# Ten quartered groups and four whole feature tiles in each feed-forward input product, instead of nine and eight

## The chip, the cores and the metric

The kernel runs on one core of one Trainium2 chip. The metric is the device time of one execution in microseconds. The engines are named as in the profile: PE (TensorE, matrix multiplication; PEld is its weight load), DVE (VectorE), ACT (ScalarE), POOL (GpSimd) and SP (SyncE, which here only issues DMAs). L604 means line 604 of the kernel before the change.

## The reference

Two layers work on 512 tokens of 1,024 features. Each has two feed-forward blocks (FFN) around a mixer, and a gated embedding at its end:

```python
def swiglu_ffn(x, w_in, w_out):
    g, u = jnp.split(x @ w_in, 2, axis=-1)
    return (jax.nn.silu(g) * u) @ w_out
...
    for i in range(DEPTH):
        h = h + 0.5 * swiglu_ffn(rms_norm(h, ffn1_norm[i]), ffn1_w_in[i], ffn1_w_out[i])
        ...
        h = h + jnp.concatenate([y_ssd, y_mla.astype(y_ssd.dtype)], axis=-1) @ w_out_mix[i]
        h = h + 0.5 * swiglu_ffn(rms_norm(h, ffn2_norm[i]), ffn2_w_in[i], ffn2_w_out[i])
        gate = jax.nn.sigmoid(rms_norm(h, ple_norm[i]) @ w_ple_gate[i])
        h = h + gate * (p[i] @ w_ple_proj[i])
    return rms_norm(h, final_norm)
```

`w_in` is 1,024 x 5,632: 2,816 columns for g and 2,816 for u. `w_out` is 2,816 x 1,024. All is float32. The change touches the input product `x @ w_in` of the four FFNs alone.

## The kernel before

**Layout.** Activations lie transposed: features on the 128 partitions, the 512 tokens along the free dimension. The 1,024 features of h are eight row tiles; g and u have 22 feature tiles of 128 columns each.

**Three matmuls for one.** Every operand is split into a high and a low half (float32r), and a product is three matmuls: high by high, high by low, low by high. A weight tile is split by one cast on ACT (L306) and one subtraction on DVE (L307), activations in `halves` by L443 and L444. Weights are loaded by SP into six raw buffers (L289); three pairs of buffers take the split ones. `weights` hands out the next unit and calls the splits of the two units after it.

**Whole tiles.** `whole(x, f)` multiplies one feature tile of g or u in the plain way: eight row tiles, three matmuls each of 512 columns (L430 to L432), 24 matmuls into one bank.

**Groups by quarters.** Four feature tiles at a time can be made with seven products instead of eight (Winograd's form of Strassen's scheme): the weight columns, the rows and the tokens are each cut in two. `product(bank, n, p, first)` is one of the seven, p from 1 to 7: four row tiles, two feature tiles and three matmuls of 256 columns (L604 to L606), 24 in all. Products 1, 2 and 4 take the normalised input itself. Products 5, 3, 6 and 7 take sums of its quarters, which `norm.sums(j)` makes for row tiles 2j and 2j + 1 (L560 to L566 on DVE, with two scaled copies on ACT, L551, and the halves of four results). On the weights' side, product 5 takes product 1's raw weights plus another quarter (an addition on DVE, L318); product 6 takes product 5's raw weights plus product 3's (L318 again); product 4 takes product 6's, and product 7 product 3's, with a further quarter added while it is loaded (an accumulating DMA on POOL's queue, L323). So the weights of 5, 6, 4 and 7 depend on earlier ones in the same buffer. Product 3 accumulates into product 5's bank, product 6 into product 1's, and 7 and 4 into the bank after 6. Results are combined on DVE (L633), with copies on ACT (L628), and `finish` multiplies by the norm's factor and applies SiLU (g, L620 and L621), or multiplies with the finished g (u, L624).

**Order of an FFN's input product.** Four whole tiles of g; the norm's statistics (L502, from the sum of squares that L490 and L491 make), their spread over the partitions (L526, L528) and the first results' evacuation (L671, L675) lie between, and one `sums(j)` after each whole tile. Then nine groups: u 0 to 3, then g and u in turn for tiles 4 to 7 and so on up to 16 to 19. `ORDER` gives the order of the products in a group; products 7 and 4 are put off into the next group. At the end, around the last group's products 7 and 4, g 20, g 21, u 20 and u 21 go whole. Each finished pair of hidden tiles is split into halves (`split_pair`) as early as buffers allow (`presplit`), the last by `split_last`. The output product follows: eight tiles, each in three pieces of 8, 8 and 6 hidden tiles (L769, L776, L778).

**What sets the order on the engines.** The calls in the code do not fix it alone: the framework that builds the program (`schedule_with_timeline_sim=True`, L1583) puts each engine's instructions in order by its own estimate of when they are ready, earlier calls first among the ready. On the chip each engine then works in that order.

## Time and profile before

| what | us |
|---|---|
| median of three runs | 2308.51 |
| lowest and highest | 2308.25 and 2312.47 |
| the profiled execution | 2306.83 |
| its span, first to last instruction | 2305.1 |

| engine | busy us | share of the span |
|---|---|---|
| PE | 2278.3 | 99% |
| DVE | 1563.9 | 68% |
| ACT | 1094.2 | 47% |
| POOL | 212.9 | 9% |

A row of a timeline has the start in us, the time taken, the engine, the line, the operation, what it writes and reads by the names in the code with its shape, and how many of the same kind follow one another; behind it in brackets stands the idle time of the engine before it and what ended that. A row of the waits has who waited for whom, the total in us, how often, and the longest. A row of the windows has a stretch, its length, each engine's busy time in it with its instructions, PE's granted clock, and what the DMA engines did. In the costliest groups: count, busy us, mean ns of one, then the idle time before them and its cause.

### The profile page before, as it was taken

What the parts mean: (1) busy time and instruction counts of PE and PEld (TensorE: products, weight loads), DVE (VectorE), ACT (ScalarE), POOL (GpSimd) and SP (SyncE); (2) the same over time, 40 slices, a digit from 0 to 9 for tenths busy, and PEclk for the clock granted to TensorE, in tenths of its full rate; (3) what the DMA queues carried; (4) which work ended last, traced back from release to release, by engine and by line L of the source; (5) the groups of instructions that cost most, each with busy time, mean ns of one, the idle gap of its engine ahead of it and who ended that gap; (6) DMA issues with size and microseconds to landing.
All of it is one profiled execution on the core that took longest, in us unless ns stands there. A gap on an engine that the chain in (4) does not pass through costs nothing.

```text
span 2305.1 us, 34208 instructions
## 1 busy us (share of the span) xinstructions
PE 2278.3 (99%) x13542; PEld 2010.8 (87%) x13542; DVE 1563.9 (68%) x2456; ACT 1094.2 (47%) x1780; POOL 212.9 (9%) x208
## 2 busy tenths in 40 slices
PE   8999999999999999999999999999999999999998
PEld 7999888888888899988899998888788889998887
DVE  7878445688676877733777773476876778776345
ACT  7456324455454645522554552254544555454224
POOL 1110001132000111000011100012310001110000
PEclk9999999999999999999999999999999999999999
DMA  6666334311222566623356652332112126664232
GB/s 173 160 155 154 89 98 114 87 43 51 62 66 74 135 156 159 151 76 89 105 130 157 161 140 84 104 106 78 35 45 83 59 78 156 162 159 119 87 87 74
DMA packets 360428, 247.89 MB, mean 108 GB/s; under 512 B 20590, under 2 KB 354636, under 8 KB 360268
## 3 DMA queue, kind: packets, MB, share of 16 engines
q1 hardware_dynamic: 322252, 207.96, 30.4%
q0 software_dynamic: 38016, 37.75, 10.8%
q8 instruction: 106, 1.74, 0.3%
q14 instruction: 54, 0.44, 0.1%
HBM read 243.58 MB, written 2.10 MB: 107 GB/s over the span
## 4 chain that ended last, share of the span: by engine, by line
PE 70%; issue 23%; DVE 3%; DMA 1%; ACT 1%; SPq 1%; POOL 1%; POOLq 0%; DVEq 0%; ACTq 0%
PE b L432 15%; PE b L430 15%; PE b L431 14%; PE b L606 5%; PE b L604 5%; PE b L605 5%; PE b L439 1%; PE b L438 1%; PE b L440 1%; DMA raw<-in_ffn_w_in_dram 1%; PE b L1126 1%; DVE lo L307 1%; PE b L1291 1%; PE b L1110 0%; PE b L502 0%
## 5 line engine op out<-in xcount | busy, mean ns | idle before, releaser
L306 ACT CAST hi<-raw 128x1024 fp32r<-128x1024 f32 (+3 forms) x536 | 524.2, 979 | 838.7 <-PE b L431 411.3
L307 DVE TENSOR_TENSOR lo<-raw,hi 128x1024 fp32r<-128x1024 f32 (+3 forms) x536 | 613.6, 1145 | 405.6 <-ACT hi L306 403.9
L430 PE MATMUL b<-s,hi 128*128 128x512 f32 (+1 forms) x1754 | 692.4, 397 | 6.0 <-ACT hi L306 5.9
L432 PE MATMUL b<-s,lo 128*128 128x512 f32 (+1 forms) x1754 | 684.5, 391 | 3.9 <-DVE lo L307 3.9
L431 PE MATMUL b<-s,hi 128*128 128x512 f32 (+1 forms) x1754 | 683.1, 390 | 0.0
L604 PE MATMUL b<-s,hi 128*128 128x256 f32 x2016 | 569.8, 283 | 1.6 <-ACT hi L306 1.6
L605 PE MATMUL b<-s,hi 128*128 128x256 f32 x2016 | 569.7, 283 | 0.0
L606 PE MATMUL b<-s,lo 128*128 128x256 f32 x2016 | 565.2, 284 | 0.0
L430 PEld LDWEIGHTS b<-s,hi 128*128 128x128 f32 x1754 | 329.8, 188 | 75.0 <-ACT hi L306 8.9
L432 PEld LDWEIGHTS b<-s,lo 128*128 128x128 f32 x1754 | 329.2, 188 | 74.7 <-DVE lo L307 6.6
L604 PEld LDWEIGHTS b<-s,hi 128*128 128x128 f32 x2016 | 387.3, 192 | 3.4 <-ACT hi L306 2.9
L431 PEld LDWEIGHTS b<-s,hi 128*128 128x128 f32 x1754 | 329.7, 188 | 67.6 <-issue 2.9
L605 PEld LDWEIGHTS b<-s,hi 128*128 128x128 f32 x2016 | 387.3, 192 | 0.3
L606 PEld LDWEIGHTS b<-s,lo 128*128 128x128 f32 x2016 | 384.5, 192 | 0.2
L323 POOL DMA_DIRECT2D raw<-in_ffn_w_in_dram x72 | 92.7, 1287 | 586.2 <-DVE lo L307 567.7
L516 POOL TENSOR_TENSOR nr<-nv,half 128x4 f32<-128x4 f32 (+1 forms) x14 | 18.3, 1304 | 1041.0 <-DVE nv L508 921.7
L443 ACT CAST s<-b 128x128 fp32r<-128x128 f32 (+2 forms) x196 | 66.9, 361 | 99.8 <-DVE s L444 33.8
L443 ACT CAST s<-s 128x256 fp32r<-128x256 f32 (+1 forms) x248 | 94.5, 423 | 32.4 <-DVE s L624 15.8
L444 DVE TENSOR_TENSOR s<-s,s 128x256 fp32r<-128x256 f32 (+1 forms) x248 | 99.7, 447 | 4.5 <-ACT s L443 4.0
L444 DVE TENSOR_TENSOR s<-b,s 128x128 fp32r<-128x128 f32 (+2 forms) x196 | 75.3, 402 | 32.2 <-ACT s L443 30.9
L318 DVE TENSOR_TENSOR raw<-raw,raw 128x1024 f32<-128x1024 f32 x72 | 88.1, 1224 | 1.8
L438 PE MATMUL b<-hi,s 128*128 128x512 f32 (+1 forms) x208 | 78.1, 375 | 0.0
(245 smaller groups left out, 2248.0 us busy)
## 6 DMA issues: line engine op xcount, KB each, us to landing
raw<-in_ffn_w_in_dram SPq DMA_DIRECT2D x176, 512.0 KB
raw<-in_ffn_w_in_dram POOLq DMA_DIRECT2D x72, 512.0 KB, 5.9
raw<-in_ffn_w_out_dram SPq DMA_DIRECT2D x64, 512.0 KB
raw<-in_w_in_mix_dram SPq DMA_DIRECT2D x50, 512.0 KB
raw<-in_w_out_mix_dram SPq DMA_DIRECT2D x32, 512.0 KB
raw<-in_ffn_w_out_dram SPq DMA_DIRECT2D x32, 384.0 KB
raw<-in_w_ple_gate_dram SPq DMA_DIRECT2D x16, 512.0 KB
raw<-in_w_q_b_dram SPq DMA_DIRECT2D x16, 192.0 KB
```

Of the source, the lines that this page charges most:

```text
L306: A.copy(hi[:, :n], x[:, :n])
L307: V.tensor_tensor(lo[:, :n], x[:, :n], hi[:, :n].bitcast(F32), op=ALU.subtract)
L323: lambda dst, src: G.dma_start(out=dst, in_=src, accum_op=ALU.add))
L430: mm(b, lhsT=hi[:, kk, cs], rhs=xh, start=st, stop=False)
L431: mm(b, lhsT=hi[:, kk, cs], rhs=xl, start=False, stop=False)
L432: mm(b, lhsT=lo[:, kk, cs], rhs=xh, start=False, stop=en)
L438: mm(b, lhsT=xh[:, cs], rhs=hi[:, kk], start=first, stop=False)
L443: A.copy(hi, src)
L444: V.tensor_tensor(lo, src, hi.bitcast(F32), op=ALU.subtract)
L604: mm(o, lhsT=hi[:, k, cs], rhs=xh, start=first and f == k == 0, stop=False, **more)
L605: mm(o, lhsT=hi[:, k, cs], rhs=xl, start=False, stop=False, **more)
L606: mm(o, lhsT=lo[:, k, cs], rhs=xh, start=False, stop=f == 1 and k == 3, **more)
```

## The change

The groups become ten: g 2 to 5, u 0 to 3, g 6 to 9, u 4 to 7, and so on to g 18 to 21 and u 16 to 19. Only g 0 and g 1 go whole at the beginning, and u 20 and u 21 at the end, around the last group's products 7 and 4. The sums for row tiles 4 to 7 are called after the second whole tile, behind the spread and the evacuation. In the first group product 2 comes before product 5 instead of after it. The g of the last pair of tiles is now made in a group, so u 20 and u 21 are multiplied into it as they come (`last_evac`), and the last pair is split like the others; `presplit` is called seven times around the end instead of ten, and counts with all 22 tiles.

```diff
-GROUPS = [("u", 0)] + [(x, q) for q in range(1, KF // 4) for x in "gu"]
+GROUPS = [(x, f + 2 * (x == "g")) for f in range(0, KF - 2, 4) for x in "gu"]
...
-FIRST_ORDER = ((1, 0), (5, 0), (2, 0), (3, 0), (6, 0))
+FIRST_ORDER = ((1, 0), (2, 0), (5, 0), (3, 0), (6, 0))
...
-        for f in range(4):
+        for f in range(2):
             whole("g", f)
         for n in range(NG):
             for p, back in ORDER if n else FIRST_ORDER:
                 quarter_unit(n - back, p)
         quarter_unit(NG - 1, 7)
-        whole("g", LAST)
+        whole("u", KF - 2)
         quarter_unit(NG - 1, 4)
-        whole("g", LAST + 1)
-        whole("u", LAST)
-        whole("u", LAST + 1)
+        whole("u", KF - 1)
...
-                if q < done[0] and len(slots.free) - 4 - (LAST - len(hid[0]) * 2) >= KEEP:
+                if q < done[0] and len(slots.free) - 4 - (KF - len(hid[0]) * 2) >= KEEP:
...
-        for f in range(4):
+        def last_evac(f, b):
+            for a in range(2):
+                x = hid[a][-1][:, f * HT:(f + 1) * HT]
+                V.tensor_tensor(x, b[:, a * HT:(a + 1) * HT], x, op=ALU.mult)
+            banks.put(b)
+
+        for f in range(2):
             held.append((f, whole("g", f)))
             if f == 0:
                 start()
                 norm.stats()
-            if f == 2:
-                norm.spread()
-            if f >= 2:
-                while held:
-                    evac(*held.pop(0))
             norm.sums(f)
+        norm.spread()
+        while held:
+            evac(*held.pop(0))
+        norm.sums(2)
+        norm.sums(3)
...
-                    done[0] = (n + 1) // 2 * 2
+                    done[0] = n // 2 * 2
...
-        g = [whole("g", LAST)]
+        b = whole("u", KF - 2)
+        last_evac(0, b)
         presplit(2)
         product(ba, NG - 1, 4, False)
         finish(NG - 1, 1, 0, ba.ap)
         banks.put(ba)
-        done[0] = LAST // 2
-        presplit(1)
-        g.append(whole("g", LAST + 1))
+        done[0] = KF // 2 - 1
         presplit(2)
-        for f in range(2):
-            t = S()
-            V.tensor_tensor(t.ap, g[f].ap, norm.rb.ap, op=ALU.mult)
-            banks.put(g[f])
-            A.activation(t.ap, t.ap, AF.Silu)
-            b = whole("u", LAST + f)
-            if f:
-                norm.drop(rb=False)
-            V.tensor_tensor(t.ap, b.ap, t.ap, op=ALU.mult)
-            banks.put(b)
-            hid[f].append(t)
-            presplit(2)
...
+        b = whole("u", KF - 1)
+        norm.drop(rb=False)
+        last_evac(1, b)
+        done[0] = KF // 2
+        presplit(2)
```

## The prediction, on record before the changed kernel was timed

> **What bounds the kernel now.** I read the page first (busy shares, granted clock, chain), then PE's waits, then the timelines of PE and DVE at the four places where an FFN (a feed-forward block) begins, and at one where its input product ends.

> ```profile
> PE 2278.3 (99%) x13542; PEld 2010.8 (87%) x13542; DVE 1563.9 (68%) x2456; ACT 1094.2 (47%) x1780; POOL 212.9 (9%) x208
> PEclk9999999999999999999999999999999999999999
> PE 70%; issue 23%; DVE 3%; DMA 1%; ACT 1%; SPq 1%; POOL 1%; POOLq 0%; DVEq 0%; ACTq 0%
> PE b L430 <- ACT hi L306: 5.9, 6, 1.4
> PE b L432 <- DVE lo L307: 3.9, 7, 1.3
> PE b L1526 <- DMA s<-in_x_dram: 3.6, 3, 1.6
> ```

> PE is busy for 99% of the span at an undiminished clock and makes up most of the chain; its longest wait is 1.6 us, its waits for weight splits (ACT's high half, DVE's low half) 10 us in all. So it is PE's work that counts, unless another engine falls behind it somewhere. What PE takes is read from rhythms, since its matmuls overlap and their mean times do not add:

> ```profile
> 825.26 1.23 DVE L318 TENSOR_TENSOR raw<-raw,raw 128x1024 f32<-128x1024 f32 x1
> ...
> 845.42 1.23 DVE L318 TENSOR_TENSOR raw<-raw,raw 128x1024 f32<-128x1024 f32 x1
> ...
> 1009.01 0.69 DVE L776 SCALAR_TENSOR_TENSOR raw<-b,s 128x512 f32<-128x512 f32 x1 [1.96 <-PE b L432]
> ...
> 1023.97 0.69 DVE L776 SCALAR_TENSOR_TENSOR raw<-b,s 128x512 f32<-128x512 f32 x1 [1.96 <-PE b L432]
> ```

> The first two rows are the same step of two neighbouring groups: a group of seven products, 7 x 24 = 168 matmuls of 256 columns, takes 20.16 us, 120.0 ns a matmul, 2.88 us a product. The other two are output tiles of 22 x 3 = 66 matmuls of 512 columns: 14.96 us, 226.7 ns a matmul, so a whole feature tile (24) takes 5.44 us.

> **The change on PE.** Each of four FFNs loses four whole tiles (21.76 us) and gains a group (20.16 us): 1.60 us less, 6.4 us in all. That is what seven products for eight leave once the narrow matmul pays its extra: two of 256 columns take 240.0 ns against 226.7 for one of 512.

> [...]

> **What rides along.**

> ```profile
> L307 DVE TENSOR_TENSOR lo<-raw,hi 128x1024 fp32r<-128x1024 f32 (+3 forms) x536 | 613.6, 1145 | 405.6 <-ACT hi L306 403.9
> L323 POOL DMA_DIRECT2D raw<-in_ffn_w_in_dram x72 | 92.7, 1287 | 586.2 <-DVE lo L307 567.7
> raw<-in_ffn_w_in_dram POOLq DMA_DIRECT2D x72, 512.0 KB, 5.9
> core 0: us, PE busy (x) PEld busy (x) DVE busy (x) ACT busy (x) POOL busy (x), PEclk, DMA share, GB/s
> 739.00:772.00 33.00, 30.80 (x133) 24.36 (x132) 33.00 (x62) 25.25 (x46) 0.00 (x0) 1.00 0.30 93
> 28.60:41.70 13.10, 11.24 (x57) 8.95 (x56) 13.10 (x30) 8.14 (x17) 0.00 (x0) 1.00 0.38 121
> 1155.00:1182.00 27.00, 27.00 (x141) 23.02 (x140) 19.79 (x34) 14.42 (x23) 1.92 (x1) 1.00 0.32 101
> 949.40:985.40 36.00, 34.75 (x176) 29.29 (x175) 23.39 (x40) 17.61 (x32) 0.00 (x0) 1.00 0.43 125
> ```

> A group brings seven weight splits for the four of the whole tiles, two additions of weights (L318), four loads on SP for four that go, and two accumulating loads on POOL's queue (72 become 80; 1.3 us to issue, 5.9 to land). In a steady group all of this is hidden: the 20.16 us is exactly the matmuls' time, and the added group is one more such. Its cover is the product of the neighbour group that runs meanwhile; it is missing at the end of the last group, as before. I cost it at nothing; uncovered, a landing would cost up to its 5.9 us once per FFN.

> At the end two whole tiles instead of four lie around the last two products, and only eight of eleven pairs of hidden tiles are split into halves in call order before the output product starts. The first matmul that needs the other three comes two whole tiles, two products and two output pieces (each 5.44 us) after the last group, 27.5 us, plus the wait that stands there now:

> ```profile
> PE b L430 <- ACT hi L306: 0.7, 1, 0.7
> PE b L432 <- DVE lo L307: 0.5, 1, 0.5
> ...
> 963.25 1.77 DVE L444 TENSOR_TENSOR s<-s,s 128x256 fp32r<-128x256 f32 x5
> ```

> DVE was busy 23.39 of the 36.00 us that follow the last group now, and loses two weight splits (2 x 1.145). It fits with 6 us to spare, so I cost this end at nothing. If the order defeats that, three pairs, 12 subtractions of 0.35 us (five take 1.77), cost up to 4 us per FFN. A gain is bounded by the 1.2 us of those two waits.

> **Where it can lose: the beginning.** Product 5 needs sums of the normalised input from all eight row tiles, each a chain of DVE and ACT steps, and its own weights, made by an addition (L318), a cast and a subtraction. Today PE has four whole tiles and product 1 to do meanwhile; after the change two whole tiles and products 1 and 2. Nothing can overtake product 5 on PE: product 3 accumulates into its bank, product 6 takes its raw weights, the next group follows. After product 5 begins, the changed kernel has 144 narrow matmuls more and 48 wide ones less to run, 17.28 - 10.88 = 6.4 us. So product 5 must begin 6.4 us earlier than now to break even, and 8.0 us earlier for the full 1.60 us.

> ```profile
> 768.41 1.23 DVE L307 TENSOR_TENSOR lo<-raw,hi 128x1024 fp32r<-128x1024 f32 x1
> 769.54 0.77 DVE L444 TENSOR_TENSOR s<-s,s 128x256 fp32r<-128x256 f32 x2
> 770.21 0.70 DVE L491 TENSOR_TENSOR s<-s,raw 128x512 f32<-128x512 f32 x1
> 770.81 1.23 DVE L318 TENSOR_TENSOR raw<-raw,raw 128x1024 f32<-128x1024 f32 x1
> ...
> 774.07 1.00 PE L502 MATMUL b<-ones,s 128*128 128x64 f32 x8
> 774.89 0.37 PE L605 MATMUL b<-s,hi 128*128 128x256 f32 x1
> 775.09 0.28 PE L606 MATMUL b<-s,lo 128*128 128x256 f32 x1
> ```

> This is the second FFN of layer 0. The row at 775.09 is the 15th of product 1's 24 matmuls, so product 5 begins 10 x 0.12 later, at 776.3, and must begin by 769.9. But DVE has no idle moment from 739 to 772 (33.00 of 33.00 above). When it is done, at 772.04, it has made all sums, the weights up to product 1's (768.41) and product 5's addition. The changed order gives it one subtraction less up to there (g0, g1, products 1 and 2 for g0 to g3 and product 1; 1.13 us from row to row), to 770.9, and then product 5's own 1.13, since its split is called after the last sums: 772.0. (Product 2, now ahead of product 5, leaves its result to an addition on DVE that is called after that split and stands behind it.) The low half is needed for the third matmul only: 771.8, 1.9 us late. That is the upper bound. The lower is no wait, -1.6. I take the upper bound less what product 1's subtraction overtook in these rows, two steps of the sums and one of the squares (769.54 to 770.81, 1.27 us): +0.6. The same FFN of layer 1 has the same order: +1.2 together.

> ```profile
> 23.23 0.69 DVE L491 TENSOR_TENSOR s<-s,raw 128x512 f32<-128x512 f32 x1
> 28.56 0.22 DVE L789 CAST pf<-pos_i 4x128 f32<-4x128 int32 x1 [4.63 <-DMA pos_i<-in_positions_dram]
> ...
> 41.30 0.40 DVE L444 TENSOR_TENSOR s<-s,s 128x256 fp32r<-128x256 f32 x1
> ...
> 42.09 1.00 PE L502 MATMUL b<-ones,s 128*128 128x64 f32 x8
> 42.90 0.37 PE L604 MATMUL b<-s,hi 128*128 128x256 f32 x1
> ```

> In the first FFN product 5 begins at 42.90; break-even is 36.5. DVE stands 4.63 us for a small load, then works without a gap (13.10 of 13.10) until the last sum at 41.70. By the same steps product 5 would start at 41.5, 5.0 us late. If moved weight work fills the 4.63 us, 0.4 late; a wholly free start is -1.6. Between 0.4 and 5.0 no row is nearer; I take the middle, 2.7.

> ```profile
> 1163.93 0.99 DVE L444 TENSOR_TENSOR s<-s,s 128x256 fp32r<-128x256 f32 x2
> 1167.91 1.23 DVE L307 TENSOR_TENSOR lo<-raw,hi 128x1024 fp32r<-128x1024 f32 x1 [2.99 <-ACT hi L306]
> ```

> At the first FFN of layer 1 the sums end by 1164.9, DVE idles 2.99 us, and PE is busy 27.00 of 27.00 us: no backlog, so the full -1.6 (at worst 0).

> **The sum.** -1.6 + 1.2 + 2.7 = +2.3 us. The profiled execution took 2306.83 (span 2305.1 and 1.7 around it), which gives 2309.1; the median of the runs is 2308.51, 1.68 higher, and so 2310.8. A measurement tells a change from none beyond about 0.2%, 4.6 us: I forecast no difference, 2304 to 2313 for this case.

> **Rivals.**
> (1) The starts do not lose: ACT and DVE slip product 5's split in among the sums (for it: they overtake already at 768.41; against: DVE has no gap there). Then 4 x -1.6 = -6.4: 2302.1.
> (2) Slower: DVE, which works through its queue in order, does all sums before product 5's subtraction. Both bounds hold: -1.6 + 2 x 1.9 + 5.0 = +7.2: 2315.7. It decides once that subtraction ends over 1 us past 771 in the second FFN, or at 40 or later in the first. For it speaks the call order; against it only the row at 768.41.
> (3) The clock falls. In the forecast's first FFN PE is through with what precedes product 5 at 34.9 (1.6 ahead of break-even) and waits until 39.2: 4.3 us, longer than any wait now (1.6), and no row shows what that does to the clock. [...]

> **Chances.** Forecast 0.43; (1) 0.27, because the margin between it and the forecast is in the order of a queue that I cannot see; (2) 0.25; (3) 0.05. So faster 0.27, same 0.43, slower 0.30. The range goes from just below (1) to just above (2): 2301.5 to 2317. It leaves out a late end of the input product and a start better than free.

> **What would show it.** 2016 matmuls of L604 become 2240 with the group's rhythm still 20.16 us. At the second FFN's start product 5 should begin near 770.5 with a wait of PE for a split just before; in the first FFN near 39.2 after some 4 us of idle PE; none at layer 1's first FFN. If PE waits there for nothing, (1) is right; if product 5 starts after 771.8 or 41.5, or the output product waits for hidden tiles, I am wrong on the other side.

## The result, and the profile after

The changed kernel took 2323.11 us, median of four runs (2321.68 to 2326.61), beside 2310.06 for the kernel before in the same comparison (2308.25 to 2312.47): ratio 1.0060, 95% interval 1.0048 to 1.0071. It is slower by 0.6%, about 13 us. The forecast was no difference, 2310.8, with a range up to 2317. The profiled executions have spans of 2305.1 and 2321.5 us: 16.4 apart, more than the medians, since that of the kernel before (2306.83) is the shortest of 26 (median 2310.45), and the longer ones have a lower mean granted clock (0.996 to 0.998 from 2310.44 us on). Lines of the changed kernel are three lower around the splits (L303 the cast, L304 the subtraction, L315 the addition of weights) and the products (L601 to L603); the whole tiles are L427 to L429, `sums` L557 to L563, the halves L440 and L441, the squares L488, the statistics L499.

From the page of after, the engines and PE's granted clock:

```profile
PE 2280.3 (98%) x13830; PEld 2025.6 (87%) x13830; DVE 1594.9 (69%) x2496; ACT 1112.8 (48%) x1812; POOL 223.2 (10%) x216
PEclk9999999999999999999999999999999999999999
```

PE is still busy for 98%, and in tenths of full speed the clock looks untouched. Neither row tells anything: the loss lies in a few spots of some microseconds. PE's waits in after (total, times, longest) show it first:

```profile
PE b L601 <- ACT hi L303: 10.1, 9, 2.3
PE b L603 <- DVE lo L304: 7.2, 5, 2.5
PE b L427 <- ACT hi L303: 3.9, 4, 1.7
PE b L429 <- DVE lo L304: 2.1, 4, 0.5
```

The products now wait 17.3 us for their splits, up to 2.5 us at a time. Before, they waited 1.6 us in all:

```profile
PE b L604 <- ACT hi L306: 1.6, 3, 0.5
```

To place the loss I took, for every matmul of a product or a whole tile, the time from its start to the next start beyond 0.1200 or 0.2267 us: gaps over 0.25 us are waits, smaller ones are slow matmuls. Each FFN is counted from 20, 740, 1140 or 1880 us, so with the end of the mixer in front of it. The end of an FFN is its last output tile on DVE (L776, after: L760). First and last start of that line, before and after:

```profile
L776 DVE SCALAR_TENSOR_TENSOR raw<-b,s x32: 691/692/693, 261.5 to 2236.2; 128x512 f32<-128x512 f32 x32
```

```profile
L760 DVE SCALAR_TENSOR_TENSOR raw<-b,s x32: 691/692/692, 269.6 to 2252.6; 128x512 f32<-128x512 f32 x32
```

| FFN | waits, us | slow matmuls, us | fewer matmul us | sum | its end moved by |
|---|---|---|---|---|---|
| first, layer 0 | 3.74 to 11.39 | 1.23 to 3.65 | -1.60 | +8.5 | +8.1 |
| second, layer 0 | 4.26 to 7.48 | 1.11 to 2.88 | -1.60 | +3.4 | +3.3 |
| first, layer 1 | 1.69 to 2.85 | 0.54 to 0.52 | -1.60 | -0.5 | -0.5 |
| second, layer 1 | 4.30 to 8.77 | 1.11 to 3.80 | -1.60 | +5.6 | +5.4 |

The sums explain the whole 16.4 us within 0.6: 16.5 us more of waits, 6.9 us of matmuls at a slower rhythm, 6.4 us saved. In the two second FFNs 3.1 to 3.2 us of the added waits and 1.7 to 1.8 of the slowness lie at the beginning; in layer 1 another 1.28 and 0.95 lie at the end of the input product.

The second FFN of layer 0 in after, PE's timeline (start, time taken; in brackets the idle time and what ended it):

```profile
771.57 0.39 PE L601 MATMUL b<-s,hi 128*128 128x256 f32 x1
771.79 0.28 PE L602 MATMUL b<-s,hi 128*128 128x256 f32 x1
773.00 0.39 PE L601 MATMUL b<-s,hi 128*128 128x256 f32 x1 [0.93 <-ACT hi L303]
773.22 0.28 PE L602 MATMUL b<-s,hi 128*128 128x256 f32 x1
775.96 0.39 PE L603 MATMUL b<-s,lo 128*128 128x256 f32 x1 [2.46 <-DVE lo L304]
...
776.84 0.41 PE L602 MATMUL b<-s,hi 128*128 128x256 f32 x1
777.05 0.41 PE L603 MATMUL b<-s,lo 128*128 128x256 f32 x1
...
782.84 1.00 PE L499 MATMUL b<-ones,s 128*128 128x64 f32 x8
783.65 0.37 PE L601 MATMUL b<-s,hi 128*128 128x256 f32 x1
```

The first pair of rows is product 2, the second product 5; both run out of operands after two matmuls, and PE stands until product 2's low half is there at 775.9. Behind the wait the matmuls come every 0.21 us instead of every 0.12. DVE at that place:

```profile
769.25 1.23 DVE L315 TENSOR_TENSOR raw<-raw,raw 128x1024 f32<-128x1024 f32 x1
770.39 0.77 DVE L441 TENSOR_TENSOR s<-s,s 128x256 fp32r<-128x256 f32 x2
771.06 0.69 DVE L488 TENSOR_TENSOR s<-s,raw 128x512 f32<-128x512 f32 x1
771.66 1.43 DVE L441 TENSOR_TENSOR s<-s,s 128x256 fp32r<-128x256 f32 x4
...
774.67 1.23 DVE L304 TENSOR_TENSOR lo<-raw,hi 128x1024 fp32r<-128x1024 f32 x1
775.81 0.70 DVE L488 TENSOR_TENSOR s<-s,raw 128x512 f32<-128x512 f32 x1
776.41 2.37 DVE L304 TENSOR_TENSOR lo<-raw,hi 128x1024 fp32r<-128x1024 f32 x2
...
782.96 1.24 DVE L304 TENSOR_TENSOR lo<-raw,hi 128x1024 fp32r<-128x1024 f32 x1
```

DVE has no idle moment from 747.1 to 784.2. The addition of weights that the prediction feared (L315) is early; product 2's subtraction (774.67) is late, behind twelve steps of sums and squares, and those of products 5 and 3 follow at 776.41. Product 6's, at 782.96, is late as well: PE works on product 6 ahead of product 3 (which needs product 5's bank, copied at 784.97 by ACT), and product 6's first matmul with a low half starts at 784.25, 0.05 us after that subtraction ends. The granted clock in after, by windows (length, busy times with instructions, clock, DMA share, GB/s), and the same time in before:

```profile
32.30:39.20 6.90, 5.95 (x29) 5.81 (x28) 6.90 (x13) 5.13 (x12) 0.00 (x0) 0.51 0.24 78
776.40:779.90 3.50, 3.50 (x19) 3.50 (x18) 3.50 (x7) 1.04 (x2) 0.00 (x0) 0.51 0.49 150
1916.50:1919.90 3.40, 3.40 (x19) 3.40 (x18) 3.40 (x7) 0.88 (x2) 0.00 (x0) 0.50 0.53 159
2114.50:2117.90 3.40, 2.88 (x7) 2.31 (x8) 3.40 (x8) 2.78 (x7) 0.00 (x0) 0.50 0.65 190
```

```profile
776.40:779.90 3.50, 3.50 (x32) 3.50 (x31) 1.98 (x3) 2.14 (x3) 1.89 (x2) 1.00 0.50 159
```

The clock halves at four of the places with new waits (0.50 and 0.51 in these windows), for 3.4 us or twice that; in 3.5 us PE starts 19 matmuls instead of 32 there. Not every new wait has this behind it: the one of 1.20 us in the first FFN of layer 1, at 1189.0, has none (1.00 from 1185 to 1200).

### The profile page after: what moved, and what is told of

It reads as the page before. It is cut to its first block, busy times and chain, and to the rows that moved or that the text cites. A ratio compares the mean times of both kernels' runs of the same rounds, so it can differ in the third digit from the quotient of the medians.

```text
span 2321.5 us, 34922 instructions
## 1 busy us (share of the span) xinstructions
PE 2280.3 (98%) x13830; PEld 2025.6 (87%) x13830; DVE 1594.9 (69%) x2496; ACT 1112.8 (48%) x1812; POOL 223.2 (10%) x216
## 3 DMA queue, kind: packets, MB, share of 16 engines
q8 instruction: 108, 1.77, 0.3%
## 4 chain that ended last, share of the span: by engine, by line
PE 58%; issue 33%; DVE 3%; DMA 2%; POOL 1%; ACT 1%; SPq 1%; POOLq 0%; ACTq 0%
PE b L429 15%; PE b L427 15%; PE b L428 15%; DMA raw<-in_ffn_w_in_dram 2%; PE b L435 2%; PE b L436 2%; PE b L437 2%; POOL raw L320 1%; PE b L1110 1%; DVE lo L304 1%; PE b L1275 1%; ACT hi L303 0%; PE b L1301 0%; PE b L1251 0%; PE b L1248 0%
## 5 line engine op out<-in xcount | busy, mean ns | idle before, releaser
L303 ACT CAST hi<-raw 128x1024 fp32r<-128x1024 f32 (+3 forms) x548 | 536.9, 981 | 842.6 <-PE b L428 390.8
L304 DVE TENSOR_TENSOR lo<-raw,hi 128x1024 fp32r<-128x1024 f32 (+3 forms) x548 | 628.1, 1147 | 416.0 <-ACT hi L303 411.9
L601 PE MATMUL b<-s,hi 128*128 128x256 f32 x2240 | 636.2, 285 | 11.7 <-ACT hi L303 10.1
L427 PE MATMUL b<-s,hi 128*128 128x512 f32 (+2 forms) x1626 | 641.9, 397 | 3.9 <-ACT hi L303 3.9
L603 PE MATMUL b<-s,lo 128*128 128x256 f32 x2240 | 630.1, 285 | 7.4 <-DVE lo L304 7.2
L429 PE MATMUL b<-s,lo 128*128 128x512 f32 (+2 forms) x1626 | 635.0, 391 | 2.1 <-DVE lo L304 2.1
L602 PE MATMUL b<-s,hi 128*128 128x256 f32 x2240 | 634.4, 284 | 0.0
L428 PE MATMUL b<-s,hi 128*128 128x512 f32 (+2 forms) x1626 | 633.4, 390 | 0.0
L601 PEld LDWEIGHTS b<-s,hi 128*128 128x128 f32 x2240 | 432.5, 193 | 15.7 <-ACT hi L303 13.3
L603 PEld LDWEIGHTS b<-s,lo 128*128 128x128 f32 x2240 | 429.4, 193 | 9.1 <-DVE lo L304 8.9
L602 PEld LDWEIGHTS b<-s,hi 128*128 128x128 f32 x2240 | 432.3, 193 | 0.6
L429 PEld LDWEIGHTS b<-s,lo 128*128 128x128 f32 (+1 forms) x1626 | 305.5, 188 | 67.3 <-DVE lo L304 4.2
L427 PEld LDWEIGHTS b<-s,hi 128*128 128x128 f32 (+1 forms) x1626 | 305.7, 188 | 66.8 <-ACT hi L303 4.7
L428 PEld LDWEIGHTS b<-s,hi 128*128 128x128 f32 (+1 forms) x1626 | 305.6, 188 | 62.6 <-issue 2.9
L440 ACT CAST s<-b 128x128 fp32r<-128x128 f32 (+2 forms) x196 | 67.1, 362 | 99.7 <-DVE s L441 33.8
L440 ACT CAST s<-s 128x256 fp32r<-128x256 f32 (+1 forms) x256 | 94.1, 416 | 27.2 <-DVE s L620 10.6
L315 DVE TENSOR_TENSOR raw<-raw,raw 128x1024 f32<-128x1024 f32 x80 | 98.0, 1225 | 6.4 <-DMA raw<-in_ffn_w_in_dram 4.2
L441 DVE TENSOR_TENSOR s<-s,s 128x256 fp32r<-128x256 f32 (+1 forms) x256 | 100.6, 438 | 1.4 <-ACT s L440 0.7
L441 DVE TENSOR_TENSOR s<-b,s 128x128 fp32r<-128x128 f32 (+2 forms) x196 | 75.3, 402 | 32.2 <-ACT s L440 30.9
L513 POOL TENSOR_TENSOR nr<-nv,half 128x4 f32<-128x4 f32 (+1 forms) x14 | 19.2, 1373 | 722.8 <-DVE nv L505 722.1
## 6 DMA issues: line engine op xcount, KB each, us to landing
raw<-in_ffn_w_in_dram SPq DMA_DIRECT2D x176, 512.0 KB
raw<-in_ffn_w_in_dram POOLq DMA_DIRECT2D x80, 512.0 KB, 5.9
raw<-in_ffn_w_out_dram SPq DMA_DIRECT2D x64, 512.0 KB
raw<-in_w_in_mix_dram SPq DMA_DIRECT2D x50, 512.0 KB
raw<-in_w_out_mix_dram SPq DMA_DIRECT2D x32, 512.0 KB
raw<-in_w_ple_gate_dram SPq DMA_DIRECT2D x16, 512.0 KB
```

Source lines behind the costliest of these rows:

```text
L303: A.copy(hi[:, :n], x[:, :n])
L304: V.tensor_tensor(lo[:, :n], x[:, :n], hi[:, :n].bitcast(F32), op=ALU.subtract)
L427: mm(b, lhsT=hi[:, kk, cs], rhs=xh, start=st, stop=False)
L428: mm(b, lhsT=hi[:, kk, cs], rhs=xl, start=False, stop=False)
L429: mm(b, lhsT=lo[:, kk, cs], rhs=xh, start=False, stop=en)
L440: A.copy(hi, src)
```

## The experiments

The theory after the result, called B: at the beginning of an FFN DVE's queue is the bound, and the change takes away 10.88 us of whole-tile work per FFN that ran while DVE caught up. Rivals: the split buffers (product 2 must wait until g 0 has left one of three pairs), the order of products or of sums, the half clock, and in the first FFN DVE's stop for a small load. Letters of theories belong to the expectation that they stand in. Ratios are to the kernel before on the same chip, in brackets their 95% intervals.

**Order of the first products.**

```diff
-FIRST_ORDER = ((1, 0), (2, 0), (5, 0), (3, 0), (6, 0))
+FIRST_ORDER = ((1, 0), (5, 0), (2, 0), (3, 0), (6, 0))
```

> The changed kernel with the first group's old order, product 5 ahead of product 2. If product 5's sums are what is late (as the prediction had it), PE waits longer, 2 to 3 us more at each of three FFNs: 2328 to 2332. If product 2's and 5's weight splits are late together (A, C), the order of the two makes no difference: within 3 us of 2323.

2323.26 us, 1.0054 (1.0039 to 1.0070). The swap of products 2 and 5 makes no difference that can be measured, for either sign.

**Sums for row tiles 4 to 7 called between products 2 and 5.**

```diff
-        norm.sums(2)
-        norm.sums(3)
...
+                    if n == 0:
+                        norm.sums(2)
+                        norm.sums(3)
                     bb = B()
                     product(bb, n, 5, True)
```

> The changed kernel, with the sums for row tiles 4 to 7 called between products 2 and 5 of the first group, so that the weight splits of products 2, 5 and 3 stand ahead of those sums in call order. Theory A (the splits of products 2 and 5 stand behind the sums in DVE's order, and that order makes PE wait): at both second FFNs the 5.5 us that PE waits in products 2 and 5 falls under 3 us, the clock stays whole there, and the time falls by 4 to 8 us against the changed kernel, to 2315 to 2319. Rival B (DVE has too much to do in total, the order only moves the wait): the wait turns up at product 5, 3 or 6 and the time stays within 3 us of 2323. Rival C (the cast of product 2's weights waits for a buffer that product 1 releases): the cast stays where it is, and only DVE's 3 us behind it go.

2322.00 us, 1.0052 (1.0034 to 1.0071). In the second FFNs the trace has the same steps on DVE in the same order, so this try did not move what it was to move, presumably because the framework puts ready steps first wherever they are called. It decides nothing.

**Useless work for PE.** 24 discarded wide matmuls per FFN (all but layer 1's first), and then 12 (with `norm.ops[4:]`):

```diff
+        if (i, nm) != (1, "f1"):
+            b = B()
+            for k, (xh, xl) in enumerate(norm.ops[:8]):
+                for x in (xh, xl, xh):
+                    mm(b.ap, lhsT=ident_r, rhs=x, start=True, stop=True)
+            banks.put(b)
         cur = {}
```

> The changed kernel with 24 matmuls of 512 columns more (5.44 us of PE), called behind the second whole tile in three of the four FFNs (not in the first FFN of layer 1); their result is thrown away. If the loss at the beginning is PE standing idle (all theories of the start), they lie in the wait: at the two second FFNs the time stays within 1 us or falls by up to 1.7 us each, because the clock need not drop; in all 2318 to 2325. If PE's own work sets the time there, 3 x 5.44 us come on top: 2339.

2322.34 us, 1.0052 (1.0036 to 1.0068): 3 x 5.44 = 16.3 us of added matmuls cost nothing. At the second FFNs' beginnings waits and slow matmuls fall from 8.4 us to 2.4 and 2.8 (same count as above), by about as much as the added work, and the clock stays whole there (1.00 from 745 to 801 in layer 0).

> The changed kernel with 12 discarded wide matmuls (2.7 us of useless PE work, half of those tried before) between g 1 and product 1 in all FFNs but the first of layer 1. Theory K (the half clock costs time of its own): the waits for product 2's split shrink from 3.7 to about 1 us, the clock does not fall there, and the 1.7 us that the half clock took come back in each second FFN, more useless work making the kernel faster: 2317 to 2320. Rival: the half clock falls into time that PE would have waited anyway, and DVE sets the pace until product 6: 2322 to 2324.

2323.78 us, 1.0057 (1.0044 to 1.0069). The waits shrink by 2.4 us (5.8 to 3.4 in each second FFN), but the clock still falls to 0.50, from 777.2 and from 1917.3. So the expected gain did not come, and the half clock could not be taken away by itself: the 24 matmuls that kept it up took as long as wait and half clock together. What it costs alone stays open.

**Three whole tiles at the beginning.** u 20 goes whole after g 1 and is kept in a slot; u 21 stays at the end:

```diff
+        b = whole("u", KF - 2)
+        first = S()
+        A.copy(first.ap, b.ap)
+        banks.put(b)
         norm.spread()
...
-        b = whole("u", KF - 2)
-        last_evac(0, b)
+        last_evac(0, first)
+        slots.put(first)
```

> The changed kernel with tile 20 of u whole at the beginning instead of at the end (its result kept in a buffer), so three whole tiles at the beginning and one at the end. If cover at the beginning is what is missing, the waits of 5.5 us at the second FFNs and the clock's drops there go, the first FFN loses 3 to 5 us less, and the time is 2304 to 2311, under or at the kernel before. Rival: the end lacks the cover instead, products 7 and 4 wait for their accumulating loads (up to 5.9 us per FFN), and the time is 2315 or more.

2311.55 us, 1.0001 (0.9992 to 1.0011): one whole tile moved to the beginning takes the loss back in the sum, though not the saving. The ends of the FFNs stand +3.7, +3.2, -1.0 and -0.9 us against before, each by itself. So the second FFN of layer 0 gets nothing back: PE's 3.7 us of waits at products 2 and 5 become 1.3 us there, at products 1 and 2, but it then waits 0.8 us for product 6's cast (781.49) and 1.65 us for POOL's step of the norm (L513, at 783.64), and the clock is at 0.50 from 783.6 to 787.0.

**Four at the beginning**, none at the end (u 21 moved likewise):

```diff
+        firsts = []
+        for f in range(2):
+            b = whole("u", KF - 2 + f)
+            t = S()
+            A.copy(t.ap, b.ap)
+            banks.put(b)
+            firsts.append(t)
...
```

> Ten groups as in the changed kernel, but g 0, g 1, u 20 and u 21 all go whole at the beginning, u 20 and u 21 kept in two slots until the last g is there; none goes whole at the end. Theory: the loss is the missing cover at the beginning, and four whole tiles give all of it back, so that the 1.6 us that each FFN's matmuls save come through, less one wait at an end that now has only products 7 and 4: 2305 to 2308, faster than before. Rival: the saving does not exist on the chip (the group's narrow matmuls cost it elsewhere, or the uncovered end takes over 2 us in each FFN): 2311 or more.

2327.92 us, 1.0077 (1.0063 to 1.0091): slower still, so the theory of this try failed. Its first half held: at the second FFN's beginning PE waits 3.0 us in all as it did before (2.7). But now the end of every input product is bare. PE's timeline there, layer 0's second FFN, and ACT's:

```profile
976.13 0.28 PE L603 MATMUL b<-s,lo 128*128 128x256 f32 x1
981.50 0.79 PE L427 MATMUL b<-s,hi 128*128 128x512 f32 x1 [5.08 <-ACT hi L303]
```

```profile
975.57 0.71 ACT L440 CAST s<-s 128x256 fp32r<-128x256 f32 x2
976.18 0.63 ACT L618 ACTIVATE s<-s 128x512 f32<-128x512 f32 x1
976.71 2.84 ACT L440 CAST s<-s 128x256 fp32r<-128x256 f32 x9
979.45 1.99 ACT L303 CAST hi<-raw 128x1024 fp32r<-128x1024 f32 x2
```

The output product's weights wait behind the halves of the last hidden pairs, which the whole tiles at the end used to hide: 5.2 to 6.6 us in each FFN, and in layer 0's two the clock is at 0.50 for 6.8 to 6.9 us with it (242.5 to 249.3 and 979.8 to 986.6).

**Buffers of their own for product 2's split** (four slots in the first group of each FFN). In this kernel's rows the lines are 19 higher, and L316 is the new subtraction.

```diff
...
+        if units[j][0][1] in ("f1", "f2") and units[j][0][2:] == (0, 2):
+            parts = [(S(F32R), S(F32R)) for _ in range(2)]
+            for s, (h, l) in enumerate(parts):
+                xs = x[:, s * 512:(s + 1) * 512]
+                A.copy(h.ap, xs)
+                V.tensor_tensor(l.ap, xs, h.f, op=ALU.subtract)
...
```

> The changed kernel, with two buffers of their own (four slots) for the split weights of product 2 in the first group of every FFN, so that its cast no longer waits until g 0's last matmul has left one of the three split pairs. Theory A (the buffer): product 2's cast and subtraction come before the last sums, PE's 1.08 and 2.62 us there go and with them the half clock behind them; what is left is a wait of some 2 us for product 5's split. Each second FFN and the first FFN of layer 0 lose about 3 us less: 2314. Theory B (DVE's whole queue): the work that DVE has to do before product 5 is the same, so the wait moves from product 2 to product 5 in full and product 5 ends where it does now: 2321 to 2323.

2322.46 us, 1.0051 (1.0038 to 1.0063): nothing gained. DVE, then PE:

```profile
766.40 1.28 DVE L316 TENSOR_TENSOR s<-raw,s 128x512 fp32r<-128x512 f32 x2
...
775.64 1.22 DVE L323 TENSOR_TENSOR lo<-raw,hi 128x1024 fp32r<-128x1024 f32 x1
```

```profile
773.39 0.28 PE L621 MATMUL b<-s,hi 128*128 128x256 f32 x1
776.91 0.58 PE L622 MATMUL b<-s,lo 128*128 128x256 f32 x1 [3.23 <-DVE lo L323]
```

Product 2's subtraction now comes at 766.40, some eight microseconds earlier, and PE waits 3.23 us for product 5's instead of 0.93 and 2.46. That is theory B's forecast: the buffer decides which product waits, not how long.

**DVE's queue made shorter, first try: the squares added on POOL.**

```diff
-                V.tensor_tensor(self.acc.ap, self.acc.ap, sq[:, :T], op=ALU.add)
+                (G if isinstance(self, NormQ) else V).tensor_tensor(self.acc.ap, self.acc.ap, sq[:, :T], op=ALU.add)
```

> The changed kernel, with the seven additions of squares ahead of each FFN made on POOL instead of DVE (0.6 us of DVE each; POOL took 1.44 us for an addition of this size elsewhere). Theory B (what PE waits for is DVE's queue as a whole): four or five of them lie in DVE's unbroken queue ahead of product 2's subtraction, so that it comes 2.4 to 3 us earlier, most of the wait goes and the half clock with it: 2.5 to 4 us less at each second FFN and at the first: 2313 to 2317. Rival: the order (sums ahead of the split) or ACT's casts hold the split whatever DVE has less to do, or POOL's slower additions delay the statistics: 2321 or more.

2335.32 us, 1.0108 (1.0095 to 1.0122), 12 us slower than the change alone. POOL, then DVE:

```profile
759.97 4.73 POOL L488 TENSOR_TENSOR s<-s,raw 128x512 f32<-128x512 f32 x2 [4.02 <-ACT raw L487]
766.26 2.94 POOL L488 TENSOR_TENSOR s<-s,raw 128x512 f32<-128x512 f32 x2 [1.56 <-ACT raw L487]
```

```profile
761.76 1.79 DVE L466 SCALAR_TENSOR_TENSOR s<-s,vec,s 128x512 fp32r<-128x512 f32 x1
763.47 1.51 DVE L563 TENSOR_TENSOR s<-s 128x256 f32<-128x256 f32 x1
764.91 0.74 DVE L466 SCALAR_TENSOR_TENSOR s<-s,vec,s 128x512 fp32r<-128x512 f32 x1
...
768.01 2.28 DVE L304 TENSOR_TENSOR lo<-raw,hi 128x1024 fp32r<-128x1024 f32 x1
```

While POOL adds, single steps of DVE take some 1.05 us more (L466 0.74 and 1.79, L304 1.23 and 2.28): the edit took 0.6 us a time off DVE's queue and put more back. So this try did not make DVE's queue shorter, and what a shorter one does was still open.

**Second try: six of the seven additions of squares left out**, in the changed kernel and in the kernel before.

```diff
-                V.tensor_tensor(self.acc.ap, self.acc.ap, sq[:, :T], op=ALU.add)
+                self.nsq = getattr(self, "nsq", 1) + 1
+                if not isinstance(self, NormQ) or self.nsq == KD:
+                    V.tensor_tensor(self.acc.ap, self.acc.ap, sq[:, :T], op=ALU.add)
```

> The changed kernel without six of the seven additions of squares in each FFN's norm (only the last is made, so that the statistics still come last; the factor of the norm is then that of two row tiles instead of eight). DVE has 3.6 us less to do ahead of each FFN, and no other engine has more. Theory B (PE waits at product 2 for the end of DVE's queue): the subtraction of product 2 comes 2 to 3.6 us earlier in both second FFNs, PE's wait of 2.62 us there falls under 1 us and the half clock behind it goes: 4 us less in each, and 3 or more in the first FFN: 2311 to 2316. Rival O (the order, or ACT's casts, decide): the wait keeps its place and size, 2321 to 2323.

2309.02 us, 0.9994 (0.9985 to 1.0003): 3.6 us less of DVE work ahead of each FFN is worth 14 us in all, and the whole loss is gone in the medians.

PE in the second FFN of layer 0 (products are L603 to L605 here), and a window behind it:

```profile
767.46 0.28 PE L604 MATMUL b<-s,hi 128*128 128x256 f32 x1
768.82 0.58 PE L605 MATMUL b<-s,lo 128*128 128x256 f32 x1 [1.08 <-DVE lo L304]
```

```profile
768.80:772.20 3.40, 3.38 (x16) 3.38 (x17) 3.40 (x7) 0.41 (x1) 1.47 (x1) 0.50 0.62 191
```

The wait of 2.46 in front of product 2's low half is 1.08 here. The window shows that the clock fell all the same, to 0.50; that part of the expectation was wrong. The FFNs' ends stand +2.8, +0.7, +0.3 and +0.4 us against before, each by itself. A second thing moved with the edit: the statistics, some 0.9 us of PE, now lie at 766.35, ahead of product 2's low half, where the changed kernel has them behind product 5. So up to 0.9 us of what came back in this FFN may be theirs.

> The same omission in the kernel before (the norm's factor is then that of two row tiles). By theory B the four whole tiles already cover DVE's queue at the second FFNs, where PE waits 1.1 us in all: at most 1 us less in each of them and 1.5 in the first: 2307 to 2310. Rival: DVE's queue sets the time there too, and as much comes back as in the changed kernel: 2303 or less.

2309.06 us, 0.9998 (0.9989 to 1.0007): with four whole tiles at the beginning the same omission is worth nothing in the sum. PE's waits at the second FFNs' beginnings do shrink, from 2.7 to 1.2 us, but the clock is at 0.50 for 3.4 us in the first FFN (34.1) and twice elsewhere (494.9 and 1358.5), where the profile of before has 1.00. So it is the change that made DVE's queue cost 14 us, not the squares.

> The changed kernel with both, product 2's own split buffers and six additions of squares left out. If the buffer is a second bound that DVE's queue hides, it shows now: 2 us or more below the kernel with only the squares left out. If DVE's queue is the only one, the two are within 1 us of each other.

2310.77 us, 1.0003 (0.9995 to 1.0012). Product 2's own buffers add nothing in the sum, 1.8 us the other way by medians. By FFN it is mixed: +4.8, -2.2, -1.2 and +3.4 against before, so better than without them in the two in the middle and worse in the first and the last. A second bound behind the queue, in single FFNs, is not ruled out.

**The small loads.** Positions and `a_log` are issued ahead of the other small loads, in the changed kernel and in the kernel before:

```diff
-        later.append(lambda: nc.sync.dma_start(out=out, in_=in_))
+        (later.appendleft if first else later.append)(lambda: nc.sync.dma_start(out=out, in_=in_))
...
```

> The changed kernel, with the small loads of positions and a_log issued ahead of the other small loads, so that DVE does not stand 4.18 us for the one, nor ACT 2.1 and 2.1 us for the other, in the middle of the first FFN's sums. Theory H: the stop is part of what makes the first FFN's beginning lose 7.4 us; sums and splits come 3 to 4 us earlier and so does product 5: 2319. Rival: product 2's cast has to wait for its buffer until 27.8 us whatever DVE does, and PE's work behind it is the bound: under 1 us, 2322 to 2323. The other FFNs stay as they are under both.

2322.69 us, 1.0050 (1.0037 to 1.0063). DVE's stop of 4.18 us is gone, and the first FFN ends 1.5 us earlier than without the edit (+6.6 instead of +8.1), but the second loses as much more (+4.8 instead of +3.3), with its clock at 0.50 for 6.8 us (774.3 to 781.2) instead of 3.4.

> The kernel before, with the early small loads alone, as a base for the combined kernel that was faster than before. If these loads matter only where the start is short of cover, nothing: 2309 to 2312. If they help in themselves, DVE's 4.63 us stop in the first FFN goes and PE's 1.44 us wait there with it: 2308 to 2309.

2304.40 us (2304.17 to 2304.68, eight runs), 0.9977 (0.9966 to 0.9987): faster than both kernels. SP issues the loads at 11 to 13 us instead of at 23 to 27:

```profile
10.99 1.74 SPq L293 DMA_DIRECT2D pos_i<-in_positions_dram  x1
12.77 0.82 SPq L293 DMA_DIRECT2D a_log<-in_a_log_dram  x2
```

PE's 2.1 us of waits at the first FFN's beginning are gone; its end comes 2.65 us earlier, and that stays to the end of the span (2302.6 for 2305.1). The medians differ by 5.4; the profiles show only half of that, since the profiled execution of the kernel before is its shortest.

**Together.** Whole u 20 at the beginning, own buffers and early small loads, and the same with the squares on POOL:

> Three edits together: u 20 whole at the beginning (which alone gave the time of before), product 2's own split buffers, and the early small loads. If the buffer and the stop are causes of their own, their parts add on what whole u 20 leaves (+3.7 us in the first FFN, +3.2 in the second, -1.0 and -0.9 in the others): 2304 to 2307. If whole u 20 had already hidden both, nothing is added: 2311.

2307.92 us, 0.9987 (0.9978 to 0.9996): below the kernel before, by less than the 0.2% that the prediction set as its bound, and above the 2304.40 of the kernel before with early small loads alone (not in the same comparison). The FFNs' ends stand +0.7, +0.7, -1.5 and +0.6 us, each by itself: only the one without a backlog on DVE has its 1.6.

> Whole u 20 at the beginning, product 2's own split buffers, early small loads and the additions of squares on POOL, all four. By theory B the starts are then free of waits in all FFNs and the 1.6 us per FFN come through in full: 2303 to 2306. Rival: what is left at the starts does not hang on DVE, or POOL's additions delay the statistics and the first evacuation: 2308 or more.

2323.02 us, 1.0054 (1.0042 to 1.0067): POOL's additions cost 15 us here too.

## Why the prediction was wrong

**PE's saving: right.** L601 has 2,240 matmuls, the rhythm is 120.0 ns, and the first FFN of layer 1, the one without a backlog, gains 0.5: the 1.60 less one wait of 1.20 for a low half. That -1.6 was given there in full was 1.1 too good.

**The second FFNs' beginning: the wait was right in size, its place and its price were not.** Product 5's 24 matmuls end at 782.84, so it effectively begins 2.88 earlier, at 779.96. That FFN starts 8.14 later than in before; on the old clock this is 771.8, the upper bound of the prediction to the tenth, 1.9 late; but it came about through product 2, so that the bound is met is chance. The step that failed is the choice of +0.6 between the bounds, on the ground of one subtraction that overtook the sums at 768.41. The framework's order let sums and squares pass product 2's subtraction instead. Product 5's own weights were ready earlier than forecast (its subtraction ends at 777.6, 769.5 on the old clock), but product 2 in front of it stood and then ran at half clock (0.51). So the sign that the prediction set for rival (2), the end of that subtraction, would have spoken against (2), while the time went its way. And the break-even of 769.9 was too late: it left out that the statistics, eight matmuls and 0.81 us, stood ahead of product 5 before (774.07) and stand behind it now (782.84), and that product 6 would wait for its low half (784.25), another 0.3 to 0.5 with the slower matmuls beside it. 1.9 + 0.8 + 0.5 = 3.2; the FFN's end moved by 3.3.

**The first FFN: product 5's start was right, what follows was not.** The 49th product matmul starts at 37.8, so product 5 begins near 38; forecast was 39.2. The way there was another, though: PE's first two waits end on ACT's casts, which in ACT's order come behind its wait for the small load of `a_log`, and the half clock (0.51) from 32.3 to 39.2 lies almost wholly ahead of product 5. So this agreement is chance too.

```profile
28.36 0.21 ACT L899 ACTIVATE d_a<-a_log 128x16 f32<-128x16 f32 x1 [1.74 <-DMA a_log<-in_a_log_dram]
29.30 1.03 ACT L303 CAST hi<-raw 128x1024 fp32r<-128x1024 f32 x1
30.38 0.39 PE L601 MATMUL b<-s,hi 128*128 128x256 f32 x1 [2.32 <-ACT hi L303]
```

The step that failed is the break-even at 36.5: it put at nothing all that comes behind product 5's start. By that start this FFN was 1.5 us late; +2.7 was forecast, +8.1 came. PE waits again, 1.2 us for a cast and 0.4 for a low half at 42 to 44, 0.9 at 54 to 55 for a cast whose weights had landed late, and 1.1 for a copy on ACT; all its waits from there to the FFN's end are 4.7 us longer than before, and the statistics stand behind product 5 here too, 0.8 us. Rival (2) priced DVE's queue at 5.0 here; it too counted a single wait.

**The end of the input product, costed at nothing: wrong in one of four.** In layer 1's second FFN u 20's first matmul waits 1.87 us (1.71 of them idle) for its cast and 3.4 us at half clock (0.50) follow, 2.2 us in all. The first three ends cost nothing, as the prediction said.

**The clock, rival (3), given 5%: it happened,** in three beginnings and one end. No row of before showed what a fall costs; 6.9 us of slow matmuls came, at a clock of 0.50 and 0.51. The longest waits just ahead were of 1.71 to 2.46 us, and the forecast had 4.3 us of idle PE in the first FFN itself, so 5% was too little.

For the second FFNs the cause is shown: DVE's queue is the bound at their beginnings. A buffer that is freed moves the wait without shortening it, a shorter queue takes these FFNs from +3.3 and +5.4 to +0.7 and +0.4, and in the sum the same cut does nothing for the kernel before. For the first FFN, half of the loss, it is shown in part: the shorter queue leaves 2.8 of its 8.1 us, but the first waits there end on ACT's casts, and the shares of DVE, ACT and the late weights are not separated. How much of the 16 us the half clock adds beyond the waits stays open.

## What to carry to other kernels

Before large, slow tiles are traded for cheaper small ones, ask what else runs under them: a whole tile was 5.44 us of PE time for one weight split and no sums, and it was worth more as cover than the 1.6 us that the better algorithm saves. Compare, at each place where a stage begins or ends, the queue of the engine that prepares the operands with the PE work that is left to hide it, and remember that the same tile cannot cover both ends. A wait moves to the next consumer when only its buffer is freed; take work out of the queue to see whether it is the bound.
